# Expert weights in 8 KB runs, tokens in block order, and two pieces of work put one or two expert pairs earlier

## The chip, the core and the metric

The kernel runs on one NeuronCore of a Trainium2 chip. The metric is the device time in microseconds; the time shown is the median of three runs. One execution was also recorded by the hardware profiler; its rows are what the prediction reads.

## What is computed

Two transformer blocks over 256 tokens of width 1024, in float32. The change touches only the last stage of the second block, a mixture of 32 experts (hidden width 512, two experts chosen per token), and the final norm behind it. Cut to that:

```python
def run_block(args):
    e, tok, w = args
    xb = xt[tok]
    hid = jax.nn.silu(xb @ w_gate[e]) * (xb @ w_up[e])
    return (hid @ w_down[e]) * w[:, None].astype(xb.dtype)
...
x = x + hier_moe(rmsnorm_2(x, g_moe[l]), ...)
return rmsnorm_2(x, g_final)
```

Each expert has a gate matrix and an up matrix of 1024 x 512 (2 MB each) and a down matrix of 512 x 1024 (2 MB): 6 MB per expert, 192 MB in all, and every one of them is read once.

## The kernel before

**Earlier stages.** Attention, the first block's feed-forward and the mixer run before; a planner (class `Pace`) chooses the order of their instructions. The expert stage is written out in the order of the program, in `moe`.

**Weights.** `Experts` holds 22 slots (tiles `wm`) of 1 MB. The 192 MB come in 192 units of one slot each, in a fixed list `order`, and all are issued on SP's queue. For an expert, units q = 0 to 3 hold gate and up, units 4 and 5 hold down. Before the change a gate/up unit held 256 rows of the gate matrix and the same 256 rows of the up matrix, in two DMAs of 512 KB (`fetch`): each of the 128 partitions gets two neighbouring rows of 512 numbers, 4 KB in one run. A down unit is one DMA of 1 MB: two neighbouring rows of 1024 numbers to a partition, 8 KB in one run. A unit is loaded as soon as its slot was read for the last time; `X.load(...)` at three places of the loop says how far ahead.

**Pairs.** Experts are worked through in 16 pairs (p = 0 to 15, `NP` = 16), each with up to 64 tokens (`CAP`) per expert. The list of units is: gate/up of pair 0, then for each p gate/up of pair p + 1 and down of pair p, and at the end down of pair 14, gate/up of pair 15, down of pair 15 (its second half in four DMAs of 512 KB). The loop of `moe` for p = 0 to 13 does, on TensorE (PE):

- on even p, `gather(4)`: the columns of the chosen tokens of four experts are drawn into `xe` by matmuls with one-hot matrices `oh` (`hot`); tokens lie in `xh` and `xl`, a high and a low part of the normed input;
- `hid_T`: the hidden values of pair p (tile `sg`) are transposed to `hdT`;
- `gate_up` of pair p + 1: 32 matmuls, each of two instructions (64 in the profile's count), over eight blocks of 128 input rows (k), gate and up (c) and the two experts (j). After the first of them `between` puts in `combine` (outputs of pair p - 1 are added to the tokens, from `ys`) and `slots_T`;
- `down` of pair p: 16 matmuls, 32 instructions, then `evac` on ScalarE (ACT) and VectorE (DVE) into `ys`.

Behind the loop stand pair 14's `combine`, `hid_T`, `slots_T`, the `gather(2)` for pair 15, `down(14)`, `gate_up(15)`, then `final_gain` (16 short matmuls with `g8` that spread the last norm's weights over 128 partitions into a slot that is no longer needed), `hid_T(15)`, `down(15)`, the last `combine` and the norm.

Because a partition holds two neighbouring rows of the weights, row block k of `xe` must hold rows 2m or 2m + 1 of a group of 256; `gather` picks those from `xh` and `xl` with a stride of two, and `g_moe_rows` holds the norm's weights in the same order.

Of the kernel before, what the change touches and what calls it, by code (L numbers as in the profile page):

```python
# [18 lines left out]
F32 = mybir.dt.float32  # L19
# [77 lines left out]
def pack_small(I):  # L97
# [243 lines left out]
class Experts:  # L341
# [14 lines left out]

    def fetch(self, slot, e, q, cut=False):

        nc, I = self.K.nc, self.K.I
        one = (lambda w: w[0, e]) if isinstance(e, int) else (lambda w: w[0, e, :, :].rearrange("o k n -> (o k) n"))  # L360
        rows = lambda n, q: one(I[n])[q * 256:(q + 1) * 256, :].rearrange("(p k) n -> p k n", k=2)
        if q < 4:
            w = slot.rearrange("p (c k n) -> p c k n", k=2, c=2)
            for c, name in enumerate(("w_exp_gate_2", "w_exp_up_2")):
                nc.sync.dma_start(w[:, c], rows(name, q))
        else:
            w = slot.rearrange("p (k n) -> p k n", k=2)
            src = rows("w_exp_down_2", q - 4)
            if cut:
                return w, src  # L370
            nc.sync.dma_start(w, src)
        return w

    def load(self, upto):
        upto = min(upto, len(self.slots)) if self.early else upto
        while self.n < min(upto, len(self.order) - 2):
            self.units[self.order[self.n]] = self.fetch(self.slot(self.n), *self.order[self.n])
            self.n += 1
# [43 lines left out]
class K:  # L422
# [1411 lines left out]
    def router(self, done, ss):  # L1834
# [3 lines left out]
        R = self.rt  # L1838
        self.gm = R.tile([128, 8], F32, name="gm")
        nc.gpsimd.tensor_copy(self.gm, self.small("g_moe_rows"))  # L1840
        hT = [self.g1([128, 2, T], "hT") for _ in range(4)]
        wr = self.small("w_rt").rearrange("p (k n) -> p k n", n=36)
# [202 lines left out]
    def moe(self, A):  # L2045
# [24 lines left out]

        def gather(n, oh, parts, j0=0, ds=range(8)):


            per = 4 if n <= 2 else 2
            for d0 in ds[::per]:
                b = self.bank()[:, :per * n * CAP].rearrange("p (d s) -> p d s", d=per)
                for d in range(per):
                    q, i = (d0 + d) // 2, (d0 + d) % 2
                    mms = [(xs[t][:, q * 256:(q + 1) * 256].rearrange("p (m i) -> p i m", i=2)[:, i], t)
                           for t in range(2) for xs in parts]  # L2080
                    for m, (w, t) in enumerate(mms):
# [205 lines left out]
```

## Time and profile before

| | |
|---|---|
| median of 3 runs | 1098.84 us (1098.18 to 1101.12) |
| profiled execution, its own time | 1100.28 us |
| span of that execution, first to last instruction | 1098.5 us |
| PE busy | 1062.1 us (97%) |
| DVE, ACT, POOL busy | 504.0, 381.1, 57.3 us |
| DMA | 300.06 MB, mean 273 GB/s; from about 650 us on 412 to 416 GB/s |
| chain that ended last | PE 73%, DMA 21%, DVE 2%, ACT 2% |

The expert stage begins at about 640 us and takes the rest of the span. A busy PE includes modelled ends of matmuls, so 97% doesn't mean that PE sets every stage's time: in the later part of the expert stage the chain lies on transfers of expert weights. Every instruction is recorded at one helper line (L249), so rows are told apart by tile names: `wm,xe` is gate/up, `wm,hdT` is down, `ys,pwT` is combine, `cst,sg` is `hid_T`, `cst,oh` is `slots_T`, `ohr,xh` and `ohr,xl` are a gather, `g,cst` is `final_gain`.

### The profile page before, as it was taken

Reading aid. Unit: us, or ns where it says so; the run is one execution under the profiler, and the core shown is the slowest. Engines: PE = TensorE matmul, PEld = TensorE weight load, DVE = VectorE, ACT = ScalarE, POOL = GpSimd, SP = SyncE. Lnnn points to the kernel's source line nnn. Section 1 sums busy time; section 2 is a strip of 40 time slices with the busy share of each in tenths; the row PEclk is TensorE's granted clock in tenths of the full one; section 3 lists DMA queues with packets and bytes.
Section 4 is the critical chain, followed back from the end, with each engine's and each line's share of the span. In section 5 each row is a group of like instructions: output and inputs, shape, how many; then the busy total and the mean of one; then the engine's idle time right before and its main releaser. Section 6 shows DMA issues by size and latency. Waiting matters only on the chain.

```text
span 1098.5 us, 16788 instructions
## 1 busy us (share of the span) xinstructions
PE 1062.1 (97%) x6848; PEld 747.5 (68%) x6848; DVE 504.0 (46%) x917; ACT 381.1 (35%) x678; POOL 57.3 (5%) x85
## 2 busy tenths in 40 slices
PE   9999999999999999999999999999999988989896
PEld 8989788999999888889998753434343434333252
DVE  5777746665655667666576442212121212121021
ACT  6553546644444475566446411000000000000012
POOL 0154011000000010100000000000000000000000
PEclk9999999999999999999999999999999999999998
DMA  8354115576556445454469789999999999999993
GB/s 307 120 190 128 59 66 173 202 271 218 176 170 204 159 136 182 146 178 150 161 217 388 267 314 413 413 414 412 413 414 412 412 412 412 414 412 414 416 413 150
DMA packets 106462, 300.06 MB, mean 273 GB/s; under 512 B 6999, under 2 KB 35980, under 8 KB 98444
## 3 DMA queue, kind: packets, MB, share of 16 engines
q1 hardware_dynamic: 104924, 294.71, 71.3%
q0 software_dynamic: 1024, 3.17, 1.0%
q8 instruction: 56, 0.92, 0.3%
q10 hardware_dynamic: 432, 1.05, 0.3%
q14 instruction: 26, 0.21, 0.1%
HBM read 297.83 MB, written 1.07 MB: 272 GB/s over the span
## 4 chain that ended last, share of the span: by engine, by line
PE 73%; DMA 21%; DVE 2%; ACT 2%; issue 1%; POOL 0%; SPq 0%; ACTq 0%; DVEq 0%
PE bank L249 73%; DMA wm<-in_w_exp_up 13%; DMA wm<-in_w_exp_down 7%; ACT junk L249 1%; DVE cy L249 0%; DMA x<-in_x 0%; DVE junk L249 0%; DVE xTl L249 0%; ACT wh L249 0%; DVE x L249 0%; ACT xTh L249 0%; DVE ys L249 0%; ACT wm L249 0%; ACT ys L249 0%; DVE dp L249 0%
## 5 line engine op out<-in xcount | busy, mean ns | idle before, releaser
L249 DVE TENSOR_TENSOR wl<-wr,wh 128x1024 fp32r<-128x1024 f32 (+1 forms) x175 | 211.1, 1222 | 134.1 <-ACT wh L249 130.8
L249 PE MATMUL bank<-wm,xe 128*64 128x512 f32 x1024 | 230.7, 596 | 3.6 <-DMA wm<-in_w_exp_gate 3.1
L249 PE MATMUL bank<-xTh,wh 128*128 128x256 f32 x768 | 223.3, 291 | 0.0
L249 ACT ACTIVATE wh<-wr 128x1024 fp32r<-128x1024 f32 (+1 forms) x175 | 180.1, 1050 | 118.3 <-PE bank L249 104.6
L249 PE MATMUL bank<-xTl,wh 128*128 128x256 f32 x768 | 217.5, 283 | 0.8 <-DVE xTl L249 0.8
L249 PE MATMUL bank<-xTh,wl 128*128 128x256 f32 x768 | 217.3, 283 | 0.2 <-DVE wl L249 0.2
L249 PEld LDWEIGHTS bank<-wm,xe 128*64 128x64 f32 x1024 | 71.2, 137 | 140.9 <-issue 121.0
L249 PEld LDWEIGHTS bank<-xTh,wh 128*128 128x128 f32 x768 | 147.1, 192 | 4.6 <-issue 2.4
L249 PEld LDWEIGHTS bank<-xTl,wh 128*128 128x128 f32 x768 | 147.2, 192 | 2.3 <-DVE xTl L249 1.2
L249 PEld LDWEIGHTS bank<-xTh,wl 128*128 128x128 f32 x768 | 147.2, 192 | 0.4 <-DVE wl L249 0.4
L249 PE MATMUL bank<-wm,hdT 128*64 128x512 f32 x512 | 123.0, 603 | 14.4 <-DMA wm<-in_w_exp_down 13.7
L249 PEld LDWEIGHTS bank<-wm,hdT 128*64 128x64 f32 x512 | 38.3, 138 | 95.1 <-issue 66.4
L249 ACT ACTIVATE sg<-bank 128x512 f32<-128x512 f32 x20 | 11.9, 597 | 241.9 <-PE bank L249 241.7
L249 DVE TENSOR_TENSOR sg<-bank,sg 128x512 f32<-128x512 f32 x16 | 11.1, 691 | 165.0 <-PE bank L249 165.0
L249 DVE SCALAR_TENSOR_TENSOR ys<-bank,ws,ys 128x512 fp32r<-128x512 f32 x32 | 24.0, 751 | 124.9 <-ACT ys L249 122.9
L249 ACT ACTIVATE ys<-bank,ws 128x512 fp32r<-128x512 f32 x32 | 22.0, 688 | 131.2 <-PE bank L249 131.2
L249 POOL TENSOR_TENSOR nr<-nr,mhalf 128x2 f32<-128x2 f32 (+1 forms) x9 | 6.0, 673 | 681.7 <-DVE nr L249 681.5
L249 PEld LDWEIGHTS bank<-ys,pwT 128*128 128x128 f32 x128 | 22.7, 188 | 18.5 <-issue 11.4
L249 PE MATMUL bank<-wl,fhh 128*128 128x512 f32 x88 | 35.2, 400 | 0.0
L249 PE MATMUL bank<-ys,pwT 128*128 128x512 f32 x128 | 34.6, 410 | 0.6 <-DVE ys L249 0.6
L249 DVE TENSOR_SCALAR pwT<-bank 128x256 fp32r<-128x256 f32 x16 | 6.8, 424 | 61.2 <-PE bank L249 61.2
L249 PE MATMUL bank<-wh,fhh 128*128 128x512 f32 x88 | 34.8, 396 | 0.0
(384 smaller groups left out, 1473.8 us busy)
## 6 DMA issues: line engine op xcount, KB each, us to landing
wm<-in_w_exp_gate SPq DMA_DIRECT2D x128, 512.0 KB, 10.2
wm<-in_w_exp_up SPq DMA_DIRECT2D x128, 512.0 KB, 10.2
wm<-in_w_exp_down SPq DMA_DIRECT2D x62, 1024.0 KB, 12.6
wr<-in_w_in SPq DMA_DIRECT2D x33, 1024.0 KB, 5.2
wr<-in_w_gate_up SPq DMA_DIRECT2D x22, 1024.0 KB, 5.4
wr<-in_w_down SPq DMA_DIRECT2D x11, 1024.0 KB, 5.1
wr<-in_w_out SPq DMA_DIRECT2D x8, 1024.0 KB, 5.1
wr<-in_w_ckv SPq DMA_DIRECT2D x4, 1024.0 KB, 5.8
```

The lines of the kernel that those rows point to most:

```text
L249: r = f(*args, **kw)
```

## The change

1. **Units.** A gate/up unit is now 512 rows of one matrix: units 0 and 2 are the halves of gate, 1 and 3 the halves of up. It is one DMA of 1 MB, four neighbouring rows to a partition, 8 KB in one run. For the first two experts (`plain`) the rows go to the partitions as k, p: four runs of 2 KB.
2. **Order of matmuls.** `gate_up` goes through the first half of gate, the first half of up, then the second halves. `between` still stands at k = 2 of gate, which now comes after 4 matmuls instead of 8.
3. **Tokens.** `xh` and `xl` are stored in block order (four ACT and four DVE instructions of 512 columns in place of two each of 1024, reading `x` with a stride of four numbers), so a gather reads them without a stride. The first gather reads `x` itself and uses the weights of `g_moe` (`gm0`, one more copy on POOL).
4. **Moved.** The one-hot matrix for a gather is made one pair earlier. The gather of pair 15 moves from behind the loop into p = 13, ahead of `gate_up(14)`; `final_gain` moves from behind `gate_up(15)` to behind `gate_up(14)`.

```diff
-        rows = lambda n, q: one(I[n])[q * 256:(q + 1) * 256, :].rearrange("(p k) n -> p k n", k=2)
+        rows = lambda n, q, k: one(I[n])[q * 128 * k:(q + 1) * 128 * k, :].rearrange("(p k) n -> p k n", k=k)
         if q < 4:
-            w = slot.rearrange("p (c k n) -> p c k n", k=2, c=2)
-            for c, name in enumerate(("w_exp_gate_2", "w_exp_up_2")):
-                nc.sync.dma_start(w[:, c], rows(name, q))
+            w = slot.rearrange("p (k n) -> p k n", k=4)
+            n = ("w_exp_gate_2", "w_exp_up_2")[q % 2]
+            if plain:
+                nc.sync.dma_start(w, one(I[n])[q // 2 * 512:q // 2 * 512 + 512, :].rearrange("(k p) n -> p k n", p=128))
+            else:
+                nc.sync.dma_start(w, rows(n, q // 2, 4))
...
-            for k, c, j in [(k, c, j) for k in range(8) for c in range(2) for j in range(n)]:
+            for k, c, j in [(4 * u + i, c, j) for u in range(2) for c in range(2) for i in range(4) for j in range(n)]:
                 if between and (k, c, j) == (2, 0, 0):
                     between()
-                self.mm(g[c][H[j]], xe[:, k, j0 + j], ws_(j, k // 2)[:, c, k % 2], k == 0, k == 7)
+                self.mm(g[c][H[j]], xe[:, k, j0 + j], ws_(j, 2 * (k // 4) + c)[:, k % 4], k == 0, k == 7)
...
         for t in range(2):
-            nc.scalar.activation(xh[t], x[t], AF.Copy, scale=self.r[:, t:t + 1])
+            for u in range(2):
+                nc.scalar.activation(blocks(xh[t], u), mixed(x[t], u), AF.Copy, scale=self.r[:, t:t + 1])
...
-            if p % 2:
-                oh = hot(quad(p + 2), min(4, NE - 2 * (p + 2)))
+            if p % 2 == 0:
+                oh = hot(quad(p + 3), min(4, NE - 2 * (p + 3)))
...
+            if p == NP - 3:
+                gather(2, oh, [xh, xl])
             hd = gate_up(2, 2 * (p % 2), unit(p + 1), between)
             X.load(12 * p + 16 + NR)
+            if p == NP - 3:
+                final_gain()
             down(2, hdT, unit(p))
...
         pT = slots_T(2, pw)
-        gather(2, oh, [xh, xl])
         pw = one_hot(2, col(rk, p + 1), col(W32, p + 1))
...
         hd = gate_up(2, 0, unit(p + 1), between)
-        final_gain()
         down(2, hid_T(2, hd), unit(p + 1), True)
```

How the order of instructions moves, at the three places that the prediction speaks of.

On SP, the loads of pair 15's gate and up, before (all of it is 16 issues) and then with the change (8 issues):

```order
L249 DMA wm_5661<-in_w_exp_gate 128x1024
L249 DMA wm_5661<-in_w_exp_up 128x1024
L249 DMA wm_5660<-in_w_exp_gate 128x1024
L249 DMA wm_5660<-in_w_exp_up 128x1024
L249 DMA wm_5659<-in_w_exp_gate 128x1024
L249 DMA wm_5659<-in_w_exp_up 128x1024
```

```order
L249 DMA wm_5657<-in_w_exp_gate 128x2048
L249 DMA wm_5656<-in_w_exp_gate 128x2048
L249 DMA wm_5655<-in_w_exp_up 128x2048
L249 DMA wm_5654<-in_w_exp_up 128x2048
L249 DMA wm_5653<-in_w_exp_gate 128x2048
L249 DMA wm_6211<-in_w_exp_gate 128x2048
```

One issue now fills a whole slot with rows of one matrix, and the two experts' halves of gate come before the halves of up.

On PE, the end of `gate_up(15)` and what stands between it and `down(15)`, before and then with the change (of `gate_up` the last matmuls):

```order
L249 MATMUL bank_81<-wm_6228,xe 64x512
L249 MATMUL bank_81<-wm_6229,xe 64x512
L249 MATMUL bank_74<-wm_6228,xe 64x512
L249 MATMUL bank_74<-wm_6229,xe 64x512
L249 MATMUL bank_77<-g_6253,cst_109 128x128 x4
L249 MATMUL bank_81<-g_6253,cst_109 128x128 x4
L249 MATMUL bank_74<-cst_109,sg 128x128 x4
L249 MATMUL bank_76<-wm_6223,hdT 64x512
```

```order
L249 MATMUL bank_77<-wm_6221,xe 64x512
L249 MATMUL bank_77<-wm_6222,xe 64x512
L249 MATMUL bank_77<-wm_6221,xe 64x512
L249 MATMUL bank_77<-wm_6222,xe 64x512
L249 MATMUL bank_74<-cst_109,sg 128x128 x4
L249 MATMUL bank_76<-wm_6216,hdT 64x512
```

`final_gain` is gone from here, and the last matmuls all go to up's bank, gate's being full 8 matmuls earlier.

On PE, p = 13 with the change, from the end of `gate_up(14)` to `down(13)`:

```order
L249 MATMUL bank_81<-wm_6220,xe 64x512
L249 MATMUL bank_81<-wm_6217,xe 64x512
L249 MATMUL bank_76<-g_6237,cst_109 128x128 x4
L249 MATMUL bank_77<-g_6237,cst_109 128x128 x4
L249 MATMUL bank_81<-wm_6218,hdT 64x512
L249 MATMUL bank_81<-wm_6212,hdT 64x512
```

`final_gain` stands here now; the 32 matmuls of the gather of pair 15 stand ahead of this `gate_up`, behind `hid_T(13)`.

## Rows read from the trace of the kernel before

**Rows 1.** busy time, clock and DMA rate of three stretches

```profile
core 0: us, PE busy (x) PEld busy (x) DVE busy (x) ACT busy (x) POOL busy (x), PEclk, DMA share, GB/s
650.00:1062.00 412.00, 394.36 (x1875) 164.34 (x1872) 82.49 (x176) 37.88 (x60) 0.00 (x0) 1.00 1.02 413
1033.00:1045.00 12.00, 9.02 (x35) 2.82 (x34) 1.81 (x3) 1.37 (x2) 0.00 (x0) 1.00 1.01 421
1053.00:1065.00 12.00, 12.00 (x58) 4.88 (x56) 2.26 (x4) 1.37 (x2) 0.00 (x0) 1.00 1.03 409
```

**Rows 2.** waits of SP's queue (us in total, times, longest)

```profile
SPq L249 <- DMA wm<-in_w_exp_down: 112.2, 53, 3.0
```

**Rows 3.** order of time, SP, two loads of down (start, us, what)

```profile
776.46 4.17 SPq L249 DMA_DIRECT2D wm<-in_w_exp_down  x4
...
806.87 4.17 SPq L249 DMA_DIRECT2D wm<-in_w_exp_down  x4
```

**Rows 4.** order of time, SP, near the end: three issues of up

```profile
1035.19 0.33 SPq L249 DMA_DIRECT2D wm<-in_w_exp_up  x1
...
1050.17 0.33 SPq L249 DMA_DIRECT2D wm<-in_w_exp_up  x1
...
1060.38 0.33 SPq L249 DMA_DIRECT2D wm<-in_w_exp_up  x1
```

**Rows 5.** DMA issues from 643 us on: count, KB each, median us to landing

```profile
wm<-in_w_exp_up SPq DMA_DIRECT2D x110, 512.0 KB, 10.2
```

**Rows 6.** DMA issues of the page, part 6: two kinds of earlier weights

```profile
wr<-in_w_in SPq DMA_DIRECT2D x33, 1024.0 KB, 5.2
...
wr<-in_w_down SPq DMA_DIRECT2D x11, 1024.0 KB, 5.1
```

**Rows 7.** order of time: token parts on ACT, on DVE, first gather on PE

```profile
637.84 1.15 ACT L249 ACTIVATE xh<-x,nr 128x1024 fp32r<-128x1024 f32 x1 [0.23 <-DVE most L249]
...
641.91 2.48 DVE L249 SCALAR_TENSOR_TENSOR xl<-x,nr,xh 128x1024 fp32r<-128x1024 f32 x2
...
654.48 0.40 PE L249 MATMUL bank<-ohr,xh 128*128 128x256 f32 x1
```

**Rows 8.** order of time, PE: `hid_T` of three pairs in a row

```profile
708.15 0.65 PE L249 MATMUL bank<-cst,sg 128*128 128x128 f32 x4
...
731.91 0.75 PE L249 MATMUL bank<-cst,sg 128*128 128x128 f32 x4
...
759.74 0.65 PE L249 MATMUL bank<-cst,sg 128*128 128x128 f32 x4
```

**Rows 9.** order of time, PE, the two halves of `down(8)`

```profile
882.33 3.65 PE L249 MATMUL bank<-wm,hdT 128*64 128x512 f32 x16 [0.77 <-DMA wm<-in_w_exp_down]
887.30 3.65 PE L249 MATMUL bank<-wm,hdT 128*64 128x512 f32 x14 [1.31 <-DMA wm<-in_w_exp_down]
```

**Rows 10.** order of time, PE, the last pairs

```profile
1040.16 3.65 PE L249 MATMUL bank<-wm,hdT 128*64 128x512 f32 x14 [1.33 <-DMA wm<-in_w_exp_down]
...
1046.91 0.31 PE L249 MATMUL bank<-ohr,xh 128*128 128x128 f32 x1
...
1050.84 7.09 PE L249 MATMUL bank<-wm,hdT 128*64 128x512 f32 x32
...
1074.01 2.05 PE L249 MATMUL bank<-g,cst 8*128 8x128 f32 x16
1075.99 0.74 PE L249 MATMUL bank<-cst,sg 128*128 128x128 f32 x4
1077.42 8.78 PE L249 MATMUL bank<-wm,hdT 128*64 128x512 f32 x32 [0.69 <-ACT hdT L249]
```

**Rows 11.** order of time, DVE: product of gate and up, pair 15

```profile
1074.20 0.69 DVE L249 TENSOR_TENSOR sg<-bank,sg 128x512 f32<-128x512 f32 x1 [9.77 <-PE bank L249]
```

**Rows 12.** busy time and clock around `down(15)`, columns of rows 1

```profile
1076.00:1080.00 4.00, 3.31 (x13) 1.37 (x14) 0.00 (x0) 1.19 (x2) 0.00 (x0) 0.71 0.69 260
1080.00:1084.00 4.00, 4.00 (x20) 1.30 (x18) 0.00 (x0) 0.00 (x0) 0.00 (x0) 0.87 0.02 6
```

More of the change, by code (lines that the diff above doesn't have):

```diff
@@ L124, in pack_small @@
     P.add("final_norm", colmajor(g("final_norm_w")))
-    P.add("g_moe_rows", g("g_moe_2")[0].reshape(4, 128, 2).transpose(1, 0, 2))
+    P.add("g_moe_rows", g("g_moe_2")[0].reshape(2, 128, 4).transpose(1, 0, 2))
     return P
@@ L355, in more, with fetch @@
         self.slots += [new[i] for i in order]
-    def fetch(self, slot, e, q, cut=False):
+    def fetch(self, slot, e, q, cut=False, plain=False):
         nc, I = self.K.nc, self.K.I
         one = (lambda w: w[0, e]) if isinstance(e, int) else (lambda w: w[0, e, :, :].rearrange("o k n -> (o k) n"))
-        rows = lambda n, q: one(I[n])[q * 256:(q + 1) * 256, :].rearrange("(p k) n -> p k n", k=2)
+        rows = lambda n, q, k: one(I[n])[q * 128 * k:(q + 1) * 128 * k, :].rearrange("(p k) n -> p k n", k=k)
         if q < 4:
-            w = slot.rearrange("p (c k n) -> p c k n", k=2, c=2)
-            for c, name in enumerate(("w_exp_gate_2", "w_exp_up_2")):
-                nc.sync.dma_start(w[:, c], rows(name, q))
+            w = slot.rearrange("p (k n) -> p k n", k=4)
[4 more added lines that the diff above has]
+                nc.sync.dma_start(w, rows(n, q // 2, 4))
         else:
             w = slot.rearrange("p (k n) -> p k n", k=2)
-            src = rows("w_exp_down_2", q - 4)
+            src = rows("w_exp_down_2", q - 4, 2)
             if cut:
@@ L376, in load @@
         while self.n < min(upto, len(self.order) - 2):
-            self.units[self.order[self.n]] = self.fetch(self.slot(self.n), *self.order[self.n])
+            self.units[self.order[self.n]] = self.fetch(self.slot(self.n), *self.order[self.n], plain=self.order[self.n][0] < 2)
             self.n += 1
@@ L1838, in router @@
         R = self.rt
-        self.gm = R.tile([128, 8], F32, name="gm")
+        self.gm, self.gm0 = (R.tile([128, 8], F32, name=n) for n in ("gm", "gm0"))
         nc.gpsimd.tensor_copy(self.gm, self.small("g_moe_rows"))
+        nc.gpsimd.tensor_copy(self.gm0, self.small("g_moe"))
         hT = [self.g1([128, 2, T], "hT") for _ in range(4)]
@@ L2069, in hot, with gather @@
             return oh
-        def gather(n, oh, parts, j0=0, ds=range(8)):
+        mixed = lambda w, u: w[:, u * 512:(u + 1) * 512].rearrange("p (m i) -> p i m", i=4)
+        blocks = lambda w, u: w[:, u * 512:(u + 1) * 512].rearrange("p (i m) -> p i m", i=4)
+        def gather(n, oh, parts, plain=False):
             per = 4 if n <= 2 else 2
-            for d0 in ds[::per]:
+            for d0 in range(0, 8, per):
                 b = self.bank()[:, :per * n * CAP].rearrange("p (d s) -> p d s", d=per)
                 for d in range(per):
-                    q, i = (d0 + d) // 2, (d0 + d) % 2
-                    mms = [(xs[t][:, q * 256:(q + 1) * 256].rearrange("p (m i) -> p i m", i=2)[:, i], t)
-                           for t in range(2) for xs in parts]
+                    k = d0 + d
+                    mms = [(xs[t][:, k * 128:(k + 1) * 128], t) for t in range(2) for xs in parts]
                     for m, (w, t) in enumerate(mms):
                         self.mm(b[:, d], w, oh[:, t, :n].rearrange("p e s -> p (e s)"), m == 0, m == len(mms) - 1)
-                V.tensor_tensor(xe[:, d0:d0 + per, j0:j0 + n].rearrange("p d e s -> p d (e s)"), b,
-                                self.gm[:, d0:d0 + per, None].to_broadcast([128, per, n * CAP]), op=ALU.mult)
+                V.tensor_tensor(xe[:, d0:d0 + per, :n].rearrange("p d e s -> p d (e s)"), b,
+                                (self.gm0 if plain else self.gm)[:, d0:d0 + per, None].to_broadcast([128, per, n * CAP]), op=ALU.mult)
         def slots_T(n, pw):
@@ L2186, in moe @@
         quad = lambda p: rk[:, :, 2 * p:min(2 * p + 4, NE)]
-        gather(2, self.oh, [x])
+        gather(2, self.oh, [x], True)
         for t in range(2):
-            nc.scalar.activation(xh[t], x[t], AF.Copy, scale=self.r[:, t:t + 1])
+            for u in range(2):
+                nc.scalar.activation(blocks(xh[t], u), mixed(x[t], u), AF.Copy, scale=self.r[:, t:t + 1])
         oh = hot(quad(1), 4)
         for t in range(2):
-            V.scalar_tensor_tensor(xl[t], x[t], self.r[:, t:t + 1], xh[t].bitcast(F32), op0=ALU.mult, op1=ALU.subtract)
+            for u in range(2):
+                V.scalar_tensor_tensor(blocks(xl[t], u), mixed(x[t], u), self.r[:, t:t + 1], blocks(xh[t], u).bitcast(F32),
+                                       op0=ALU.mult, op1=ALU.subtract)
         hd = gate_up(2, 0, unit(0))
```

## The prediction

> **What bounds the kernel now.** I read the busy time of stretches first. From 650 us to 1062 us the DMA engines are never short of work: a share of 1.02 and 413 GB/s over 412 us [rows 1]. PE looks nearly as busy there (394 of 412 us), so the second look is at which of the two waits for the other. In the first third PE works without a gap: from one `hid_T` to the next it takes 731.91 - 708.15 = 23.76 us for a pair without a gather, and 759.74 - 731.91 = 27.83 us for one with it [rows 8], 25.8 us on average. A pair's transfers take 806.87 - 776.46 = 30.41 us [rows 3]. PE begins with 22 loaded slots in hand and eats them up at 4.6 us a pair; from `down(8)` at 882 us on PE waits for transfers, first 0.77 and 1.31 us in the two halves of that down [rows 9]. From then on the end of the kernel moves with the transfers, and up to there they run at full rate too, since slots come free early enough. SP itself waits for transfers: an issue goes out when the eighth one before it has landed, as the 53 waits for a down, 112.2 us in all, show [rows 2]. So the spacing of SP's issues is the spacing of landings.
>
> The rate is not the same for both kinds of weights. In 12 us of down alone it is 421 GB/s, in 12 us of gate/up alone 409 GB/s [rows 1]. On SP, six issues from 1035.19 to 1050.17, each released by a 1 MB down, take 14.98 us: 2.497 us per MB. The eight from there to 1060.38, each released by 512 KB of gate or up, take 10.21 us: 2.553 us per MB [rows 4]. The two kinds differ in the run per partition (8 KB against 4 KB) and in the size of a DMA (1 MB against 512 KB). The change gives gate/up both properties of down: also a contiguous megabyte of memory, with 8 KB to a partition.
>
> **The change, part by part.**
>
> *Units of 8 KB runs.* From 643 us on there are 110 issues of up [rows 5] and one of gate with each, 110 MB; the other 18 MB came earlier, ahead of need. By SP's spacing a megabyte gains 2.553 - 2.497 = 0.056 us, in all 6.2 us. By the two rates it gains 1.0486 MB / 409 GB/s - 1.0486 MB / 421 GB/s = 2.564 - 2.491 = 0.073 us, in all 8.0 us. I take 7.0, between them, and keep both. A pair's transfers then take 12 x 2.49 = 29.9 us.
>
> The trace itself shows that run length and size go with the rate. The Trainium skill ("DMA: Bandwidth & Descriptors", Specifications) speaks against the gain: it puts the minimum for line rate at 512 B, so that 4 KB runs would have it already. By that rule this term would be 0 and the sum -1.0 us. The rates of down and of gate/up in rows 1 disagree with it by 2.9%.
>
> *Fewer, larger DMAs in flight.* Eight issues in flight are now 8 MB, not 4 MB. That asks for slots to be free earlier, and where they are not, SP waits for PE with at least as much in flight as today. Slots come free in the same steps: two units after each 16 instructions of `gate_up`, before and after. No cost.
>
> *Runs of 2 KB for the first two experts.* Eight units, all issued before 643 us. The earlier weights bound the price: `w_in`, in runs of 2 KB, lands 5.2 us after its issue, `w_down` of the first block, in runs of 4 KB, after 5.1 us [rows 6]. 8 x 0.1 = 0.8 us of transfer, at a time when the DMA engines have gaps and PE does not yet need these units. 0, at most 0.8.
>
> *Order inside `gate_up`.* Same 64 instructions. `between` now comes 8 instructions (1.8 us) earlier after the down whose results it adds. `hid_T` and 8 instructions still lie between, about 2.5 us, and the evacuation took less than that in the trace. If a wait of some tenths is left, PE's 4.1 us of slack per pair covers it in all pairs but the last.
>
> *Parts of the tokens.* ACT takes 1.15 us for one of the two tiles `xh`, DVE 2.48 us for the two `xl`, done at 644.4 us; the gather that reads them starts at 654.5 us [rows 7]. Even at double the time per number for the stride of four, both end long before. 0.
>
> *Gather of pair 15 and `final_gain` into pair 13.* The gather takes 1050.84 - 1046.91 = 3.93 us, `final_gain` 1075.99 - 1074.01 = 1.98 us [rows 10]. Pair 13 has no gather of its own: 23.76 + 3.93 + 1.98 = 29.7 us of PE against 29.9 us of transfers. That just fits. If `gate_up(14)` must wait until DVE has emptied the gather's last bank, up to 1.0 us more (by the same step in rows 11: 0.19 us to DVE, 0.69 us, then back to PE), pair 13 ends up to 0.8 us late.
>
> What that buys at the end: today PE runs without pause from the last unit of down 13 (1040.16) to the end of `gate_up(15)` (1074.01), 33.85 us [rows 10]. The transfers need 30.46 us from that unit to pair 15's last up (1060.38 + 10.2 [rows 4, 5]), and PE then has the last matmuls to do, 14 instructions or 3.4 us after the change. So both are level today. With faster transfers the limit is 12 x 2.49 + 3.4 = 33.3 us, and PE without the gather needs 33.85 - 3.93 + 0.7 (a wait for `hdT` that the gather hid) = 30.6 us. PE has 2.7 us in hand, more than the 0.8 us it may be late. The gather's move gains nothing by itself; without it 0.6 us of the DMA gain would be lost.
>
> `final_gain` is different: it stands on the path. Today `down(15)` starts 1077.42 - 1074.01 = 3.41 us after the end of `gate_up(15)`. But `hid_T` must wait for DVE's product in any case, which ended 0.88 us after PE [rows 11]. Without `final_gain`: 1.0 + (1077.42 - 1075.99) = 2.43 us. Gain 1.0 us, bounds 0.7 and 1.4.
>
> *The clock in `down(15)`.* In the profiled execution the granted clock was 0.71 in 1076 to 1080 us and 0.87 in the next 4 us [rows 12]: 4 x 0.29 + 4 x 0.13 = 1.7 us lost, part of the time at 1.2 GHz, after PE had done `final_gain` and waited 0.69 us for `hdT`. `down(15)` took 8.78 us, `down(14)` 7.09 [rows 10]: the same 1.7 us. In the changed kernel PE idles around `hid_T` in place of `final_gain`; whether the clock falls there no row tells. I keep it as it is, and take 1.7 us off in a case of its own.
>
> **Sum.** -7.0 - 1.0 = -8.0 us. Against the profiled execution, 1100.28 us with a span of 1098.5, that is 1092.3. That execution is 1.44 us slower than the median of the runs; against the median, 1098.84 - 8.0 = **1090.8 us**. A measurement of this kernel can tell about 0.3%, 3.3 us.
>
> **Rivals.**
>
> 1. *The clock stays up in `down(15)`.* 1090.8 - 1.7 = 1089.1 us. For it: the gap now holds only idle time and `hid_T` and is 1.0 us shorter. Against it: PE waits twice there. Chance 0.20.
> 2. *PE becomes the bound near the end.* Place: pair 13, with 29.7 us against 29.9. It decides once pair 13 is more than 2.7 us late; up to 2 us beyond that gives 1091.5 to 1093. Chance 0.12.
> 3. *Half the gain.* The rate of down is owed partly to its neighbours: transfers overlap where the kinds change. 1098.84 - 3.5 - 1.0 = 1094.3 us. The 12 us of down alone speak against it. Chance 0.08.
> 4. *No gain from longer runs or larger DMAs.* Gate/up keeps its 2.553 us per MB, whatever the form: the change does not do what it says. Only `final_gain` counts: 1097.8 us. The 512 B rule of the Trainium skill, above, would give this. Chance 0.05.
> 5. *The clock falls in the waits, and the kernel is slower.* All units now come a megabyte at a time, so `gate_up` waits as down does: busy for 14 to 16 instructions, idle for 1.3 us [rows 9]. If the clock fell to 1.2 GHz in these waits, PE would lose its 29.9 - 25.8 = 4.1 us of slack. It decides from 4.1 us lost per pair on; with four falls of 1.7 us per pair, 6.8 us, the six pairs behind `down(8)` would each be 2.7 us longer: 1090.8 + 16 = 1107 us. Against it: in the 12 us of down alone PE was busy for 9.02 us only, and the clock was 1.00 [rows 1]. Chance 0.03.
>
> **How the numbers follow.** The forecast has a chance of 0.52; its own range is 1089.5 to 1092.3 (6.2 to 8.0 and 0.7 to 1.4). With rivals 1 and 2 the range is 1088.0 to 1093.8; rivals 3, 4 and 5 (0.16) lie outside. Faster by over 0.3% means below 1095.5: forecast and rivals 1 to 3, 0.92. Within 0.3%: rival 4, 0.05. Slower: rival 5, 0.03.
>
> **What would show it.** In the changed profile SP's issues of gate and up should be 2.49 us apart where their eighth predecessor is any unit; a pair's transfers 29.9 us; the DMA rate about 421 GB/s from 650 us to the end of the loads. PE's pairs in the first third should be unchanged, and its first wait for a down later than 882 us. Pair 13 should hold the gather and `final_gain`, with hardly any wait for a transfer. `down(15)` should start 2.4 us after the last up matmul. The forecast is wrong if gate/up units land 2.55 us apart, if PE waits for DVE in pair 13 so long that `gate_up(15)` ends more than 3.5 us after its last unit landed, or if the granted clock is below 1.00 before 1060 us.

## The result, and the profile after

| | before | changed |
|---|---|---|
| median, first comparison | 1098.89 us (1098.18 to 1101.12, 5 runs) | 1089.67 us (1089.56 to 1090.35, 5 runs) |
| profiled execution, own time | 1100.28 us | 1089.57 us |
| its span | 1098.5 us | 1087.8 us |

The changed kernel takes 0.9914 of the time before (95% interval 0.99 to 0.9927). Run twice more beside the experiments it had medians of 1089.41 and 1089.70 us, ratios 0.9907 (0.9893 to 0.992) and 0.9912 (0.9898 to 0.9925). The forecast was 1090.8 us in a range of 1088.0 to 1093.8.

The first view is again the busy time by stretches. The columns are those of [rows 1]: length, busy time of each engine, granted clock, DMA share, GB/s.

```profile
650.00:1055.00 405.00, 394.34 (x1906) 170.81 (x1904) 82.88 (x178) 39.08 (x62) 0.00 (x0) 1.00 1.01 421
1045.00:1057.00 12.00, 12.00 (x55) 4.89 (x52) 2.26 (x4) 1.37 (x2) 0.00 (x0) 1.00 1.01 421
1068.00:1072.00 4.00, 3.52 (x18) 1.24 (x20) 0.00 (x0) 0.43 (x1) 0.00 (x0) 1.00 0.70 261
1072.00:1076.00 4.00, 4.00 (x20) 1.44 (x17) 0.75 (x1) 1.07 (x2) 0.00 (x0) 1.00 0.03 9
```

The rate is 421 GB/s over 405 us, where [rows 1] have 413. The stretch from 1045 us holds landings of gate/up alone: 421 in place of 409. The last two lines are `down(15)`: the clock is 1.00, where [rows 12] have 0.71 and 0.87.

SP's issues tell the same by their spacing (order of time: start, length, what; one line merges a group of issues). First the downs of two pairs in a row, as in [rows 3], then the last gate/up issues, as in [rows 4]:

```profile
765.10 7.76 SPq L249 DMA_DIRECT2D wm<-in_w_exp_down  x4
...
794.92 5.30 SPq L249 DMA_DIRECT2D wm<-in_w_exp_down  x3
```

```profile
1030.24 2.81 SPq L249 DMA_DIRECT2D wm<-in_w_exp_up  x2
1035.22 2.82 SPq L249 DMA_DIRECT2D wm<-in_w_exp_gate  x2
1040.21 2.82 SPq L249 DMA_DIRECT2D wm<-in_w_exp_up  x2
1045.18 14.18 SPq L249 DMA_DIRECT2D wm<-in_w_exp_down  x6
```

A pair now takes 794.92 - 765.10 = 29.82 us, not 30.41. Near the end two units take 4.97 to 4.99 us, 2.49 us each. There each issue of gate/up was released by the landing of a down, eight issues earlier; the six issues of down behind them, released by gate/up, stand 2.47 to 2.49 us apart. So both kinds now take the same time.

The page's line on packets, before and then with the change, shows what became of the transfers:

```profile
DMA packets 106462, 300.06 MB, mean 273 GB/s; under 512 B 6999, under 2 KB 35980, under 8 KB 98444
DMA packets 91100, 300.03 MB, mean 276 GB/s; under 512 B 4951, under 2 KB 33932, under 8 KB 67724
```

There are 15,362 packets fewer. A packet of weights is one run of memory. The 120 units of experts 2 to 31 were 256 runs each and are 128 now: 120 x 128 = 15,360 fewer. Two smaller terms cancel: the eight units of the first two experts have 512 runs instead of 256 (2,048 more), and 2,048 packets of 4 bytes are gone (under 512 B: 6999 and 4951), 16 for each of the 128 DMAs that are no longer issued.

Now PE, in order of time (start, length, what, count, idle time before and what ended it). First the place where it begins to wait for weights, then pair 13 and the end:

```profile
903.41 3.22 PE L249 MATMUL bank<-wm,xe 128*64 128x512 f32 x13 [1.10 <-DMA wm<-in_w_exp_up]
...
908.38 3.65 PE L249 MATMUL bank<-wm,hdT 128*64 128x512 f32 x16 [1.32 <-DMA wm<-in_w_exp_down]
```

```profile
1010.66 1.94 PE L249 MATMUL bank<-wm,xe 128*64 128x512 f32 x8
...
1026.97 2.05 PE L249 MATMUL bank<-g,cst 8*128 8x128 f32 x16
1028.95 7.41 PE L249 MATMUL bank<-wm,hdT 128*64 128x512 f32 x32
...
1062.55 3.65 PE L249 MATMUL bank<-wm,xe 128*64 128x512 f32 x14 [1.11 <-DMA wm<-in_w_exp_up]
1067.05 0.75 PE L249 MATMUL bank<-cst,sg 128*128 128x128 f32 x4 [0.85 <-DVE sg L249]
1068.48 7.09 PE L249 MATMUL bank<-wm,hdT 128*64 128x512 f32 x32 [0.69 <-ACT hdT L249]
```

The first listed wait is at 903 us; before it was in `down(8)` at 882 us [rows 9]. In pair 13 `gate_up(14)` at 1010.66, `final_gain` at 1026.97 and `down(13)` at 1028.95 have no wait ahead of them. At 1062.55 PE waits 1.11 us for the last unit of up. `down(15)` starts at 1068.48 and takes 7.09 us, where [rows 10] have 1077.42 and 8.78. The waits for weights from 860 us on, in total (us, times, longest), before and then with the change:

```profile
PE bank L249 <- DMA wm<-in_w_exp_down: 13.7, 12, 1.4
PE bank L249 <- DMA wm<-in_w_exp_gate: 3.1, 3, 1.0
PE bank L249 <- DMA wm<-in_w_exp_up: 0.5, 3, 0.2
```

```profile
PE bank L249 <- DMA wm<-in_w_exp_down: 7.6, 6, 1.3
PE bank L249 <- DMA wm<-in_w_exp_up: 3.3, 3, 1.1
```

They are 10.9 us in 9 waits, against 17.3 us in 18 before, though transfers now set the end more clearly than then. The chain that ended last lies on DMA for 33% of the span, against 21%.

The two profiled spans differ by 10.7 us, and the rows divide this up:

| part | before | changed | difference |
|---|---|---|---|
| end of `gate_up(15)` | 1074.01 | 1066.21 | -7.80 |
| from there to the start of `down(15)` | 3.41 | 2.27 | -1.14 |
| `down(15)` on the chain of waits | 8.81 | 7.11 | -1.70 |
| rest of the span | 12.27 | 12.21 | -0.06 |

The first line is the transfers', the second `final_gain`'s, the third the clock's.

### The profile page after: what moved, and what is told of

Its sections match the earlier page's. It is cut to its first block, busy times and chain, and to the rows that moved or that the text cites. A ratio compares the mean times of both kernels' runs of the same rounds, so it can differ in the third digit from the quotient of the medians.

```text
span 1087.8 us, 16591 instructions
## 1 busy us (share of the span) xinstructions
PE 1056.4 (97%) x6848; PEld 750.9 (69%) x6848; DVE 505.7 (46%) x919; ACT 383.5 (35%) x680; POOL 57.4 (5%) x86
## 2 busy tenths in 40 slices
DMA packets 91100, 300.03 MB, mean 276 GB/s; under 512 B 4951, under 2 KB 33932, under 8 KB 67724
## 3 DMA queue, kind: packets, MB, share of 16 engines
q0 software_dynamic: 1024, 3.17, 1.0%
q10 hardware_dynamic: 432, 1.05, 0.3%
## 4 chain that ended last, share of the span: by engine, by line
PE 61%; DMA 33%; DVE 2%; ACT 2%; issue 1%; POOL 0%; SPq 0%; ACTq 0%; DVEq 0%
PE bank L249 61%; DMA wm<-in_w_exp_up 20%; DMA wm<-in_w_exp_down 13%; ACT junk L249 1%; DMA x<-in_x 0%; DVE cy L249 0%; DVE junk L249 0%; DVE xTl L249 0%; ACT wh L249 0%; DVE x L249 0%; ACT xTh L249 0%; ACT sg L249 0%; ACT wm L249 0%; DVE dp L249 0%; POOL nr L249 0%
## 5 line engine op out<-in xcount | busy, mean ns | idle before, releaser
L249 ACT ACTIVATE wh<-wr 128x1024 fp32r<-128x1024 f32 (+1 forms) x175 | 180.1, 1050 | 118.4 <-PE bank L249 102.8
L249 PEld LDWEIGHTS bank<-wm,xe 128*64 128x64 f32 x1024 | 74.7, 137 | 137.4 <-issue 123.4
L249 PE MATMUL bank<-wm,hdT 128*64 128x512 f32 x512 | 118.7, 594 | 8.9 <-DMA wm<-in_w_exp_down 7.6
L249 PE MATMUL bank<-wh,fhl 128*128 128x512 f32 x88 | 34.5, 392 | 0.0
```

What stands on the lines that cost most here:

```text
L249: r = f(*args, **kw)
```

## The experiments

Each kernel was timed beside the kernel before on the same chip. That kernel's median was 1099.67 us beside the first four (`e1` to `e4`), 1100.02 us beside `e6` to `e8`, and 1099.02 us beside `e5`, `e4b` and `e10`.

**The new units without the moves.** `e1` puts both pieces back:

```diff
-            if p == NP - 3:
-                gather(2, oh, [xh, xl])
...
-            if p == NP - 3:
-                final_gain()
...
         pT = slots_T(2, pw)
+        gather(2, oh, [xh, xl])
...
         hd = gate_up(2, 0, unit(p + 1), between)
+        final_gain()
```

> The changed kernel with the gather of pair 15 and final_gain back at their old places: the new units alone. Theory A (the transfers give most, final_gain 1.1 us, the clock 1.7 us): SP's units 2.49 us apart, DMA rate 421 GB/s, gate_up(15) ends 0.3 to 0.6 us later than in the changed kernel (the gather is on PE's path again), down(15) starts 3.4 us after it; 1089.7 + 0.5 + 1.1 = 1091.3 us, or 1093.0 if the clock falls again in down(15). Rival B (the moves do the work, by freeing PE for the transfers): about the time before less final_gain's share is gone, 1097 to 1099 us, and units 2.55 us apart or PE late for them.

Measured: 1092.51 us (1091.15 to 1092.9), ratio 0.9931 (0.9918 to 0.9944). The stretches, and PE at the end:

```profile
650.00:1055.00 405.00, 391.06 (x1878) 168.85 (x1876) 82.85 (x178) 37.91 (x60) 0.00 (x0) 1.00 1.01 421
1068.00:1072.00 4.00, 3.31 (x13) 1.35 (x14) 0.00 (x0) 1.25 (x3) 0.00 (x0) 0.74 0.65 242
1072.00:1076.00 4.00, 4.00 (x18) 1.34 (x16) 0.00 (x0) 0.00 (x0) 0.00 (x0) 0.83 0.02 7
```

```profile
1054.10 12.24 PE L249 MATMUL bank<-wm,xe 128*64 128x512 f32 x56
1066.27 2.05 PE L249 MATMUL bank<-g,cst 8*128 8x128 f32 x16
1068.24 0.74 PE L249 MATMUL bank<-cst,sg 128*128 128x128 f32 x4
1069.67 8.78 PE L249 MATMUL bank<-wm,hdT 128*64 128x512 f32 x32 [0.69 <-ACT hdT L249]
```

The rate is 421 GB/s, and `gate_up(15)` ends at 1066.27, only 0.06 us later than with the moves, where theory A asked for 0.3 to 0.6. `down(15)` starts 3.40 us later and takes 8.78 us at a granted clock of 0.74 and 0.83. Otherwise theory A holds, with the clock's case, and rival B falls: without any move, `gate_up(15)` ends 7.7 us earlier than in the kernel before.

**The moves without the new units.** `e2` makes the same moves in the kernel before, with the one-hot matrix made a pair earlier. Against the kernel before:

```diff
-            if p % 2:
-                oh = hot(quad(p + 2), min(4, NE - 2 * (p + 2)))
+            if p % 2 == 0:
+                oh = hot(quad(p + 3), min(4, NE - 2 * (p + 3)))
...
+            if p == NP - 3:
+                gather(2, oh, [xh, xl])
             hd = gate_up(2, 2 * (p % 2), unit(p + 1), between)
             X.load(12 * p + 16 + NR)
+            if p == NP - 3:
+                final_gain()
...
-        gather(2, oh, [xh, xl])
...
-        final_gain()
```

> The kernel before with the moves alone: the gather of pair 15 and final_gain in p = 13, units and matmul order as before. Theory A: the transfers set the end of gate_up(15), which stays within 0.5 us of before, down(15) starts 1.1 us earlier after it: 1098.9 - 1.1 = 1097.8 us; if it is final_gain ahead of hid_T that brings the clock down, 1.7 us more: 1096.1 us. Rival B (the moves do the work): 1091 to 1093 us. Rival C (pair 13 too full for PE): 1099 us or more.

Measured: 1097.23 us (1096.37 to 1098.15), ratio 0.9974 (0.9963 to 0.9984). The stretches and the end on PE:

```profile
650.00:1055.00 405.00, 390.37 (x1872) 164.16 (x1870) 81.03 (x174) 37.98 (x61) 0.00 (x0) 1.00 1.02 413
1076.00:1080.00 4.00, 3.52 (x18) 1.24 (x20) 0.00 (x0) 0.43 (x1) 0.00 (x0) 1.00 0.70 262
1080.00:1084.00 4.00, 4.00 (x20) 1.52 (x17) 0.75 (x1) 1.07 (x2) 0.00 (x0) 1.00 0.04 12
```

```profile
1070.13 1.08 PE L249 MATMUL bank<-wm,xe 128*64 128x512 f32 x4 [1.05 <-DMA wm<-in_w_exp_gate]
1071.40 2.79 PE L249 MATMUL bank<-wm,xe 128*64 128x512 f32 x10 [0.19 <-DMA wm<-in_w_exp_up]
1075.05 0.75 PE L249 MATMUL bank<-cst,sg 128*128 128x128 f32 x4 [0.85 <-DVE sg L249]
1076.48 7.09 PE L249 MATMUL bank<-wm,hdT 128*64 128x512 f32 x32 [0.69 <-ACT hdT L249]
```

The rate stays at 413 GB/s and `gate_up(15)` ends at 1074.2, as before: here PE waits for the last gate/up units (1.05 and 0.19 us), so the transfers set it. `down(15)` starts 2.3 us later, at full clock. The moves are worth 2.4 us in the medians and 2.7 in the spans. Theory A asked for 2.8 with the clock and 1.1 without it, and rivals B and C fall.

**What of the new form sets the rate.** Four kernels change the length of a run and the size of a DMA apart from one another. `e3` keeps 1 MB and goes back to 4 KB; tokens' parts and `g_moe_rows` are arranged to match.

```diff
-                nc.sync.dma_start(w, rows(n, q // 2, 4))
+                nc.sync.dma_start(slot.rearrange("p (g k n) -> p g k n", g=2, k=2),
+                                  one(I[n])[q // 2 * 512:q // 2 * 512 + 512, :].rearrange("(g p k) n -> p g k n", g=2, k=2))
```

> The changed kernel with gate/up units of one DMA of 1 MB, but two runs of 4 KB to a partition (rows 2p and 2p + 1 of each group of 256), tokens' parts to match. Theory A1 (the length of the run sets the rate): gate/up 2.55 us per MB as before, 409 GB/s in a stretch of gate/up alone; 1089.7 + 7 to 8 = about 1097 us. Rival A2 (the size of the DMA, or one matrix per unit, sets it): 2.49 us per MB, 421 GB/s, 1089.7 us.

Measured: 1097.61 us (1096.91 to 1097.86), ratio 0.9978 (0.997 to 0.9987).

```profile
650.00:1055.00 405.00, 390.29 (x1875) 163.82 (x1873) 81.32 (x175) 38.90 (x62) 0.00 (x0) 1.00 1.02 413
1045.00:1057.00 12.00, 11.47 (x52) 4.58 (x51) 4.09 (x13) 1.97 (x3) 0.00 (x0) 1.00 1.02 409
```

413 GB/s, and 409 in a stretch of gate/up alone, just as in [rows 1]: a larger DMA, one matrix per unit and the new order in `gate_up` bring nothing as long as the run is 4 KB. A1 holds.

`e4` keeps 8 KB and halves the DMA by partitions.

```diff
-                nc.sync.dma_start(w, rows(n, q // 2, 4))
+                for h in range(2):
+                    nc.sync.dma_start(w[64 * h:64 * h + 64], rows(n, q // 2, 4)[64 * h:64 * h + 64])
```

> The changed kernel with each gate/up unit loaded by two DMAs of 64 partitions, 512 KB each, runs of 8 KB kept. Theory A1 (the length of the run sets the rate): 2.49 us per MB, 421 GB/s, 1089.7 us within 1 us. Rival A2 (the size of the DMA sets it): 2.55 us per MB, 1097 us.

Measured: 1413.19 us in the median of six runs that lie far apart (1361.43 to 1436.27), and all of them far from either theory.

```profile
650.00:1055.00 405.00, 303.28 (x1132) 113.51 (x1128) 49.26 (x105) 22.02 (x35) 0.00 (x0) 0.86 0.96 247
900.00:1100.00 200.00, 137.48 (x464) 49.82 (x466) 21.09 (x45) 9.53 (x15) 0.00 (x0) 0.83 0.91 229
1100.00:1300.00 200.00, 141.00 (x502) 53.08 (x499) 22.13 (x46) 10.13 (x16) 0.00 (x0) 0.85 0.92 228
```

The DMA engines are busy for 0.91 to 0.96 of the time and move 228 to 247 GB/s. In the trace's packet records an 8 KB packet takes 509 ns on average and 546 in the median, against 314 in the changed kernel. So the packets themselves are slow, not their issue. One possible explanation is that lower and upper partitions are written in turn, each time by all engines at once; `e4b` takes even and odd partitions for the halves.

```diff
-                nc.sync.dma_start(w, rows(n, q // 2, 4))
+                for h in range(2):
+                    nc.sync.dma_start(w[h::2], rows(n, q // 2, 4)[h::2])
```

> The changed kernel with each gate/up unit loaded by two DMAs of 512 KB, one for the even partitions and one for the odd ones, runs of 8 KB. In the kernel with lower and upper 64 partitions an 8 KB packet took 507 ns on average (312 to 662) in place of 314. Theory P (all DMA engines wrote to the same half of the partitions at once): with even and odd partitions packets take 314 ns again, 421 GB/s, 1089.7 us within 1.5 us. Rival Q (a DMA of 64 partitions is slow wherever they lie): about 1400 us again. Rival R (512 KB a DMA costs the 0.06 us per MB): 1097 us.

Measured: 1091.10 us (1090.97 to 1091.3), ratio 0.9925 (0.991 to 0.994); packets of 314 ns.

```profile
650.00:1040.00 390.00, 378.74 (x1834) 163.97 (x1831) 78.63 (x168) 37.12 (x59) 0.00 (x0) 1.00 1.01 420
```

Theory P holds. A DMA of 64 partitions is not slow as such; one that has all its 64 partitions in the lower or the upper half is, where the two alternate as in `e4`. The Trainium skill ("SBUF — State Buffer", Door 1) says which: partitions 0 to 63 reach 8 of 16 ports for transfers, and 0 to 127 all of them. Its next section, "Can I just issue two DMAs to hit both halves?", says that only one transfer over all 128 partitions can reach all 16; 420 GB/s with two transfers of 64 speak against that.

As to size, rival R falls: `e4b` is 1091.10 - 1089.70 = 1.4 us above the changed kernel beside it, 0.013 us per MB of gate/up, a fifth of what the run brings. That is the most that 512 KB can cost, since the split by partitions may have a share in it.

`e5` goes to four runs of 2 KB in a DMA of 1 MB, for all experts, with tokens' parts and `g_moe_rows` to match:

```diff
-            self.units[self.order[self.n]] = self.fetch(self.slot(self.n), *self.order[self.n], plain=self.order[self.n][0] < 2)
+            self.units[self.order[self.n]] = self.fetch(self.slot(self.n), *self.order[self.n], plain=True)
...
-        mixed = lambda w, u: w[:, u * 512:(u + 1) * 512].rearrange("p (m i) -> p i m", i=4)
+        mixed = lambda w, u: w[:, u * 512:(u + 1) * 512].rearrange("p (i m) -> p i m", i=4)
```

> The changed kernel with gate/up units of one DMA of 1 MB, but four runs of 2 KB to a partition for all experts, tokens in plain order. Theory A1, a fixed cost per run: the DMA engines' packets are one run each, 163 ns for 4 KB and 314 ns for 8 KB, so 12 ns fixed and 37.75 ns per KB; 2 KB then takes 88 ns, 4 x 88 against 314 ns per 8 KB, 12% more: gate/up 2.79 us per MB against 2.49 (0.30 x 110 = 33 us), or, scaled from the measured difference of 4 KB and 8 KB (0.07 us per MB, twice as much again for 2 KB), 0.21 x 110 = 23 us: 1113 to 1122 us. Rival A2 (runs from 2 KB on are all the same, 8 KB alone is special): as with 4 KB, about 1097 us.

Measured: 1114.55 us (1114.07 to 1114.83), ratio 1.0138 (1.0123 to 1.0154). The whole stretch, and a hundred of its later microseconds:

```profile
650.00:1040.00 390.00, 365.31 (x1742) 153.24 (x1740) 75.88 (x161) 33.98 (x54) 0.00 (x0) 1.00 1.04 397
900.00:1000.00 100.00, 87.35 (x400) 35.77 (x398) 18.15 (x37) 8.94 (x14) 0.00 (x0) 1.00 1.04 397
```

397 GB/s, and 15 us slower than before. Theory A1 holds, near the low end of its range, and rival A2 falls.

All of it together. Packet times are means from 700 to 1050 us, in `e4` from 700 to 1380 us, of gate/up's packets, at 8 KB with down's. GB/s is the rate of all weights, of which a third is down with 8 KB runs in every kernel. The medians come from three comparisons; the changed kernel's is from that of `e5` and `e4b`.

| kernel | run, DMA | packet | GB/s | median |
|---|---|---|---|---|
| `e5` | 2 KB, 1 MB | 88.3 ns | 397 | 1114.55 |
| `e2` | 4 KB, 512 KB | 163.1 ns | 413 | 1097.23 |
| `e3` | 4 KB, 1 MB | 163.4 ns | 413 | 1097.61 |
| `e4b` | 8 KB, 512 KB, even/odd | 313.9 ns | 420 | 1091.10 |
| changed | 8 KB, 1 MB | 314.2 ns | 421 | 1089.70 |
| `e4` | 8 KB, 512 KB, lower/upper | 509.0 ns | 228 to 247 | 1413.19 |

From 4 to 8 KB a packet grows by 150.8 ns, which leaves 163.4 - 150.8 = 12.6 ns for the packet itself, whatever its length. From that, 75.4 + 12.6 = 88.0 ns is expected at 2 KB, and 88.3 was measured.

**What the moves do, and the clock.** `e6` puts back `final_gain` alone:

```diff
-            if p == NP - 3:
-                final_gain()
...
         hd = gate_up(2, 0, unit(p + 1), between)
+        final_gain()
```

> The changed kernel with final_gain alone back behind gate_up(15); the gather of pair 15 stays in p = 13. Theory A (final_gain ahead of hid_T both costs 1.1 us on the path and brings the clock down in down(15)): down(15) starts 3.4 us after the end of gate_up(15) and takes 8.8 us, granted clock below 0.9 there: 2.8 us over the changed kernel, 1092.5 us if that has 1089.7. Rival B (the clock stays up because PE waits for transfers ahead of gate_up's last matmuls, whatever stands behind them): down(15) takes 7.1 us, 1.1 us over the changed kernel, 1090.8 us.

Measured: 1090.88 us (1090.65 to 1092.15), ratio 0.9923 (0.9909 to 0.9936).

```profile
1062.54 3.65 PE L249 MATMUL bank<-wm,xe 128*64 128x512 f32 x14 [1.10 <-DMA wm<-in_w_exp_up]
1066.11 2.05 PE L249 MATMUL bank<-g,cst 8*128 8x128 f32 x16
1068.09 0.74 PE L249 MATMUL bank<-cst,sg 128*128 128x128 f32 x4
1069.52 7.09 PE L249 MATMUL bank<-wm,hdT 128*64 128x512 f32 x32 [0.69 <-ACT hdT L249]
```

```profile
1068.00:1072.00 4.00, 3.31 (x18) 1.47 (x18) 0.00 (x0) 1.19 (x2) 0.00 (x0) 1.00 0.72 269
1072.00:1076.00 4.00, 4.00 (x20) 1.29 (x18) 0.28 (x1) 0.69 (x1) 0.00 (x0) 1.00 0.03 8
```

`down(15)` starts 3.41 us after the end of `gate_up(15)`, 1.1 us later than in the changed kernel: `final_gain`'s price. PE does the same instructions in the same order as in `e1`, within 0.1 us of the same spacing, from 1066.11 to `down(15)`, and yet the clock is 1.00. Of A the first half holds, and the second doesn't in this execution. Rival B's numbers came out: 7.09 us for `down(15)` (7.1 expected) and 1090.88 us (1090.8 expected), and PE does wait here, 1.10 us ahead of the last 14 matmuls, where `e1` has no wait.

`e7` puts back the gather alone:

```diff
-            if p == NP - 3:
-                gather(2, oh, [xh, xl])
...
         pT = slots_T(2, pw)
+        gather(2, oh, [xh, xl])
```

> The changed kernel with the gather of pair 15 alone back behind the loop; final_gain stays in p = 13. Theory A (the clock goes by final_gain): the clock stays at 1.00 in down(15), which takes 7.1 us; gate_up(15) ends 0.1 us later than in the changed kernel, as with both pieces back: 0.1 us over the changed kernel, 1089.8 us; by the prediction's step 0.6 us over it. Rival B (PE without a wait for transfers ahead of down(15) loses the clock): 1.8 us over it, 1091.5 us.

Measured: 1089.82 us (1089.33 to 1089.86), ratio 0.9908 (0.9894 to 0.9921).

```profile
1053.91 12.24 PE L249 MATMUL bank<-wm,xe 128*64 128x512 f32 x56
1067.01 0.74 PE L249 MATMUL bank<-cst,sg 128*128 128x128 f32 x4 [0.87 <-DVE sg L249]
1068.44 7.09 PE L249 MATMUL bank<-wm,hdT 128*64 128x512 f32 x32 [0.69 <-ACT hdT L249]
```

No wait ahead of the last 56 matmuls, and `gate_up(15)` ends at 1066.18, against 1066.21 with the gather moved: PE and transfers end level, and moving the gather saves nothing measurable. The clock is up here too, so rival B of `e7` falls: with `final_gain` in p = 13, PE needs no wait to keep the clock.

Rows of one execution can't tell whether the clock in `e1` and `e6` differs by rule or by chance, but each timed run has its mean granted clock. In the profiled spans (`e4` left aside) the loss of 1.7 us goes with a mean of 0.995, and full clock in `down(15)` with 0.996 or 0.997. Counting runs with 0.995 or less: with both pieces at their old places 25 of 42 (before 21 of 37, `e1` 4 of 5); with `final_gain` alone back (`e6`) 1 of 5; with `final_gain` in p = 13 (changed three times, `e2`, `e3`, `e4b`, `e5`, `e7`, `e8`, `e10`) 1 of 54, a run of `e2`. Of the 19 runs of before beside the first four kernels, the ten with 0.995 have a median of 1100.8 us and the five with 0.997 one of 1098.9. So the fall comes in some executions of one and the same kernel and not in others, and it costs about 1.9 us when it comes.

The count is a rough one. The mean covers the whole span, and at the end of each of these profiled spans the clock is at half, for 5.5 to 8.2 us, so a single mean doesn't say where the clock fell. In `e2` the four runs with 0.995 or 0.996 are 0.7 to 1.8 us longer than the other three, and yet the profiled one among them (1097.60 us, 0.996) has full clock in `down(15)`.

With `final_gain` out of the way the fall hardly comes at all. Whether moving the gather alone would do as much isn't settled: `e6` lies nearer to the kernels with `final_gain` moved than to `e1`, as its rival B says, but five runs don't decide it. Why the fall comes in one execution and not the next stays open.

**Cutting the last transfers.** In the changed kernel PE has 14 instructions left after up's last landing. `e8` loads the last two units of up in four DMAs of 512 KB, first rows of both experts first.

```diff
+            if self.order[self.n] == (NE - 2, 3):
+                two = [self.slot(self.n + i).rearrange("p (k n) -> p k n", k=4) for i in range(2)]
+                for h in range(2):
+                    for i, w in enumerate(two):
...
+                        self.K.nc.sync.dma_start(w[:, 2 * h:2 * h + 2], src[:, 2 * h:2 * h + 2])
```

> The changed kernel with the last two units of up (second halves of experts 30 and 31) loaded by four DMAs of 512 KB, runs of 4 KB, so that PE has 6 to 8 instructions left after the last landing, not 14. Theory: gate_up(15) ends 1.8 us after its last landing instead of 3.7; the four DMAs cost 2 x 0.07 us; down(15) may then wait some tenths for its own weights: 1.0 to 1.7 us below the changed kernel, 1088.0 to 1088.7 us. Rival (down(15)'s own transfers set the end): no gain, 1089.7 us.

Measured: 1089.09 us (1088.98 to 1089.31), beside the changed kernel's 1089.41 (1089.2 to 1089.91) in the same comparison.

```profile
1051.43 12.88 PE L249 MATMUL bank<-wm,xe 128*64 128x512 f32 x56
1065.17 0.75 PE L249 MATMUL bank<-cst,sg 128*128 128x128 f32 x4 [0.85 <-DVE sg L249]
1066.60 7.95 PE L249 MATMUL bank<-wm,hdT 128*64 128x512 f32 x32 [0.69 <-ACT hdT L249]
```

`gate_up(15)` ends at 1064.3 and `down(15)` starts at 1066.60, both 1.8 us earlier than in the changed kernel beside it, but then it takes 7.95 us. The first down unit of the second expert lands at 1067.31, and the third instruction starts at 1067.35; in the changed kernel it landed 0.9 us ahead of `down(15)`. After that the two experts' matmuls, which otherwise start in pairs, stay out of step, and at the end of `down(15)` 0.9 of the 1.8 us are left. The spans keep 0.4 of them and the medians 0.3: the last store lands 0.9 us earlier, and the span runs on for half a microsecond more after it, which no row explains. The rival is mostly right: the theory asked for a gain of 1.0 to 1.7 us.

`e10` cuts the last DMAs of down as well.

```diff
-            for c in range(2):
+            for c, k in ((0, slice(0, 2)), (1, slice(0, 1)), (1, slice(1, 2))):
                 for w, src in two:
-                    self.K.nc.sync.dma_start(w[:, :, c * 512:c * 512 + 512], src[:, :, c * 512:c * 512 + 512])
+                    self.K.nc.sync.dma_start(w[:, k, c * 512:c * 512 + 512], src[:, k, c * 512:c * 512 + 512])
```

> The kernel with the last two units of up cut in half, and the last two DMAs of the last down cut in two as well (256 KB each, runs of 2 KB as before): after the last landing PE has 2 to 4 instructions left in place of 8. Theory (the last landings set the end of down(15), which took 7.95 us there in place of 7.09): 0.9 to 1.3 us below the kernel with up cut alone, 1.2 to 1.6 us below the changed kernel: 1087.8 to 1088.2 us where that has 1089.4. Rival (a DMA that small lands later for its size): no gain over the kernel with up cut alone, 0.3 us below the changed kernel.

Measured: 1089.08 us (1088.78 to 1089.18), beside the changed kernel's 1089.70 (1089.19 to 1090.17). `down(15)` takes 7.80 us in place of 7.95. The theory is wrong: the last landing, at 1072.89, comes well before the last instruction's start at 1074.13, and what holds `down(15)` up is again the first unit of the second expert (landed at 1067.60, third instruction at 1067.64). The rival's number came out, no gain over the first cut alone (1089.09 us), but not for the rival's reason. A cut of that unit, or that unit ahead of the last ones of up, was not tried. The first cut is 0.3 us below the changed kernel and both together are 0.6 us below it; the 95% intervals of the ratios are over 3 us wide, so neither gain is shown beyond doubt.

**The changed kernel again.** It ran beside these, as a measure for the small differences.

> The changed kernel itself, beside the other three on the same chip: 1089.7 us within 0.6 us, down(15) at the full clock in its profile again.

> The changed kernel once more, beside the other three on the same chip: 1089.5 us within 0.6 us, and mean granted clock of each run the same, as none of its executions loses the clock in down(15).

Measured: 1089.41 and 1089.70 us. All ten executions had a mean clock of 0.996 or 0.997.

## Why the prediction was right, and where it was off

- **What bounds the kernel.** Right. The end of `gate_up(15)` followed the transfers: 7.7 us earlier with the new units and no move (`e1`), no earlier with the moves alone (`e2`). The order of matmuls and tokens that goes with the units brings nothing by itself, as `e3` shows at 4 KB.
- **8 KB runs, -7.0 us.** The mechanism was right, the size off by a tenth: -7.8 us, near the bound of 8.0 that came from the two rates. The taken value leant on 2.497 us for a MB of down, from six issues near the end [rows 4]. A MB of either kind takes 29.82 / 12 = 2.485 us now, and with that the same working gives 110 x 0.068 = 7.5 us.
- **Runs of 2 KB for the first two experts, 0 to 0.8 us.** No cost shows: `gate_up(0)` starts at 640.65 us, before at 640.59. But the bound was too low: by the packet times of `e5` and `e2`, 88.3 and 163.1 ns, the eight units keep the DMA engines busy 1.7 us longer, an estimate. The time from issue to landing (5.2 and 5.1 us) didn't show that.
- **Why the runs count.** The prediction said that run length and size go with the rate, without telling them apart. It is the run: 4 KB to 8 KB is worth 7 to 8 us at 1 MB a DMA, 512 KB to 1 MB at most 1.4 us at 8 KB a run, and nothing at 4 KB (1097.23 and 1097.61 us).
- **The rival by the 512 B rule** (the Trainium skill, "DMA: Bandwidth & Descriptors", Specifications). It fell: runs of 2, 4 and 8 KB for gate/up, all above 512 B, give 397, 413 and 421 GB/s. A section of the same page that the prediction did not use, "Why small descriptors are slow (HBM only)", tells of a fixed cost of about 3 cycles per packet. A fixed cost is what the packet records show, 12.6 ns, and it is felt at 4 KB as well: 12.6 of 163.4 ns.
- **`final_gain`, -1.0 us.** Right: -1.14 in the spans, and 1.1 on PE when it is put back alone (`e6`).
- **The gather into pair 13.** It fitted, as said, without a wait. But the 0.6 us that it was to rescue are not there. With the gather back (`e7`) `gate_up(15)` ends no later. The step put 3.4 us for the matmuls behind the last landing; they take 3.66. (Its sum for the transfers of the kernel before, 30.46, should be 30.42, which changes nothing.) So the limit is 33.5 us, not 33.3, and PE's path with the gather was 33.6, not 33.85 (`e1`: 1032.65 to 1066.27).
- **The clock in `down(15)`.** This is the step that failed: it was kept at the loss of the one profiled execution, with 0.20 for the rival in which it stays up. That rival happened: the clock is 1.00 in `down(15)` of all three profiles of the changed kernel, and the mean clock is 0.996 or 0.997 in all 15 runs. The step took a state of one execution for a property of the kernel. The 1.44 us by which that execution stood above the median was already a sign of it.
- **PE's slack, rivals 2 and 5.** PE's pairs in the first third are unchanged (23.75 and 27.73 us against 23.76 and 27.83), the first wait came 21 us later, and the clock stayed at 1.00 in the waits up to 1055 us. `e5` waits more still, busy for 87 of 100 us, and keeps 1.00. What rival 5 speaks of happens in `e4`, with far longer waits: there PE waits up to 4.8 us at a time, and the granted clock is 0.83 to 0.86 over hundreds of microseconds, part of the time at 1.2 GHz.

By the measured sizes the sum against the profiled execution is -7.8 - 1.1 - 1.7 = -10.6 us, and -10.7 was measured. Against the median of the first comparison it is -9.2 us, of which the first two terms make 8.9: by this the clock cost the median of before only some 0.3 us. So it is partly luck that 1089.67 us lies so near to the 1089.1 us of rival 1. That number has 7.0 us for the transfers and 1.7 for the clock; the measured difference has 7.8 and some 0.3.

The bounds of the forecast don't quite follow from its terms: 6.2 to 8.0 and 0.7 to 1.4 give 1089.4 to 1091.9 us, not 1089.5 to 1092.3, and with rival 1 the lower end is 1087.7, not 1088.0; no working gives the upper end of 1093.8. The measured median lies inside either way.

## What to carry to other kernels

Where transfers set the end and their rate is even over hundreds of microseconds, look at the length of one run per partition before anything else: going from 4 to 8 KB gave 2% of the rate here, with no cost that the rows show. And before one execution's clock is put into a sum, see in the other runs whether it is the kernel's or that execution's; work that stands alone between two stages is worth moving into a stage that has slack, for its own time (1.1 us here) and perhaps for the clock behind it.

## What the runs showed that was not expected

- By the packet times at 2, 4 and 8 KB (88.3, 163.4, 314.2 ns), some 12.6 ns of a packet don't grow with its bytes, and the kernel's time follows: 1114.6, 1097.6, 1089.7 us. By the same line a run of 16 KB would take 616 ns against 2 x 314.2 = 628, an estimate; it was not tried, since the slots hold 8 KB a partition.
- Splitting each gate/up transfer into lower and upper 64 partitions costs 272 to 347 us here, by run; splitting it into even and odd ones 1.4 us.
- The clock in `down(15)` falls in some executions of a kernel and not in others. By the mean clock, low in 25 of 42 runs with both pieces at their old places, in 1 of 5 with `final_gain` alone there, in 1 of 54 with `final_gain` moved.
